# A two-block transformer kernel: the v projection in wide blocks, a later end of the state-space work, and 16 KB more SBUF for expert weights

## Chip, cores, metric

One Trainium2 chip, one core. The metric is the device time of one execution in microseconds (us), the median of three runs. A profile is taken of one further execution of the same program.

## What is computed

256 tokens of width 1024 pass through two blocks, all in 32-bit floats. The first block projects the normed tokens by one matrix `w_in` into eight pieces and runs a state-space branch (SSM) and a dilated attention beside each other:

```python
h = rms_norm(x, norm_w[layer])
proj = h @ w_in[layer].astype(f32)
u_s, z_s, q, k, v, z_a, r_s, r_a = jnp.split(proj, offsets, axis=-1)
y_s = s5_branch(u_s, ...)
y_s = (y_s * jax.nn.silu(z_s)) @ w_ssm_out[layer]
...
y_a = dilated_attention(q, k, v)
y_a = (y_a * jax.nn.silu(z_a)) @ w_attn_out[layer]
m = jax.nn.sigmoid(r_s) * y_s + jax.nn.sigmoid(r_a) * y_a
x = x + m @ w_o[layer]
```

q, k and v are 1536 columns wide. The second block has a gated linear recurrence, a differential attention and then a mixture of experts: 32 experts with three 1024 x 512 matrices each, two experts per token.

## The kernel before, in words

**Two regimes.** Up to about 600 us the dense projections run, then the experts. The dense weights are some 84 MB, the expert weights 192 loads of 1 MB (the last 16 of them in half size, 200 loads in the program).

**Dense weights.** All of them go through one queue of chunks (`stream`, `pull_load`, `pull_split`, `next_weights`). A chunk is 128 x 1024 numbers (512 KB). It is loaded by SP into a slot of WR, and `pull_split` then makes two halves of each number: ScalarE copies the chunk to a rounded type (hi, line 272), VectorE subtracts (lo = w - hi, line 253), each into a slot of WR of the rounded type fp32r. TensorE then takes three products (hi x hi, hi x lo, lo x hi) in place of one in full 32 bits. The keys named in `WHOLE` (before: u, k, v) are not split: `dense` multiplies the chunk as it is, one matmul per tile, which the profile shows as two records each, line 453 `d<-WR,WR`. `dense` works on one block of 256 columns. `dense_wide` (line 477), used for the keys in `WIDE`, works on two blocks at once with 512 columns per matmul; its 48 matmuls read four chunks. WR has five slots, one of 1024 columns and four of 2048, so nine places for a chunk; `make` changes a free slot's type. Two of the slots begin as 32-bit, three as fp32r.

**Work beside the projections.** SSM, the preparation of q and k (`head_prep`) and the attention are generators. `side_run` pulls them on between the chunks at the rates in `SIDE`. `side_drain` finishes one of them at the place in `ORDER` that names it: `"ssm"` stands before `"zs"`. SSM goes through four rounds (B = 0 to 3); each has three places where TensorE takes part: transposes (line 764), products with u2 (line 779), and bd and the outputs (lines 819, 833, 836). VectorE does most of the rest with instructions of 504 to 512 columns, among them scans (line 801). The order in which instructions of one engine stand is then fixed by the scheduler of the language.

**Expert weights.** `moe_load` takes the next tile of 1 MB (8 KB of each partition) if a heap has room, else it returns. While the dense projections run, `prefetch` calls it at rates `PFR` until `PF` tiles are held; later it takes all the room there is: the main heap F, a piece of the small heaps, K, four slots R and four of WR. Each group of four experts (`NG`) reads 24 tiles, eight of w1, w3 and w2 each, and gives them back four at a time (line 1867 issues the load into the room that came free).

Of the kernel before, what the change touches and what calls it, by code (L numbers as in the profile page):

```python
# [9 lines left out]
F32 = mybir.dt.float32  # L10
F32R = mybir.dt.float32r
I32 = mybir.dt.int32
AF = mybir.ActivationFunctionType
# [227 lines left out]
class Kernel:  # L241
# [781 lines left out]
    def setup(self):  # L1023
        nc, I = self.nc, self.I
        self.side, self.mid = [], []
        self.mheaps = [self.F]
        self.moe_stream()
        self.depth_load, self.depth_split = 3, 2
        self.pf_due, self.pf_rate, self.pf_limit = 0.0, 0.6, 0
        self.ring = Ring(self.keepp.tile([128, RING_COLS], F32, name="ring"), RING_COLS)  # L1030
        self.cst = self.keepp.tile([128, C_KEEP], F32, name="cst")
        self.prm = self.keepp.tile([128, P_KEEP], F32, name="prm")
        self.cst2, self.prm2 = self.K.alloc(NC_CONST - C_KEEP), self.K.alloc(NC_PAR - P_KEEP)
        self.K.sq = self.K.alloc(128)
        sq = Ring(self.K.sq.ap, 128)
        self.sq = {n: sq.take(w) for n, w in (("q", 48), ("k", 48), ("dq", 16), ("dk", 16))}
        self.epsb = self.keepp.tile([128, 1], F32, name="epsb")
        self.V.memset(self.epsb, EPS)
        self.act(self.small(1), self.epsb, AF.Tanh)
        nc.sync.dma_start(self.prm, I["prm"][:, :P_KEEP])  # L1040
        self.ident = self.con("ident")
        self.u_dram = nc.dram_tensor("u_scratch", [DM, T], F32, kind="Internal").ap()

    def first_block(self):
        nc, I, F, R = self.nc, self.I, self.F, self.R
# [60 lines left out]
        hT = []  # L1106
# [17 lines left out]
        nc.sync.dma_start(self.cst[:, 128:], I["cst"][:, 128:C_KEEP])  # L1124
        self.pull_split(raw(1))
        next(tables)
        one = self.one = self.keepp.tile([128, 1], F32, name="one")
        V.memset(one, 1.0)
        ss = self.psum("o", 2)

# [20 lines left out]
        for c in range(4):  # L1151
            ev = evac_to(uT)(c)
# [23 lines left out]
        ssm = self.ssm(u2, uT)  # L1176
# [27 lines left out]
        def shaped_ps(ps):  # L1204
            return ps.rearrange("p t (h d) -> p t h d", d=64)
# [14 lines left out]
        def last(which, c):  # L1220

            if which == WHOLE[-1] and c == 5:
                hT.extend((R.alloc(8, 256), R.alloc(8, 256)))
                self.mid.extend(halves(i) for i in range(4))

        def operand(which):
            return (hr, None) if which in WHOLE else hT

        att = None
        for which in ORDER[1:ORDER.index("so")]:  # L1230
            if which not in WHOLE:
                ssm_side[1] = SIDE[6]
            if which in ("k", "q"):
                raw = big[which]
                raw.ap = shaped(raw.ap, (12, 2, 128))
                sq = self.sq[which]
                if which in WHOLE:
                    for c in range(6):
                        last(which, c)
                        self.dense(which, *operand(which), heads(c, raw, sq), token_major=True)  # L1240
                else:
                    for c in range(3):
                        self.dense_wide(which, *hT, heads2(c, raw, sq))
                preps[which] = self.head_prep(which, raw.ap, sq)
                self.side_add(preps[which], SIDE[1])
                trans[which] = raw
            elif which == "v":
                v = big["v"]
                v.ap = shaped(v.ap, (2, 24, 64))
                for c in range(6):  # L1250
                    def ev(ps, c=c):
                        self.scaled_tok(v[:, :, c * 4:c * 4 + 4], shaped_ps(ps))
                    last("v", c)
                    self.dense("v", *operand("v"), ev, token_major=True)
            elif which in width:
                g = gate[which] = F.alloc(width[which], 256)
                for c in range(width[which] // 2):
                    self.dense(which, hT[0], hT[1], (silu2 if which[0] == "z" else tanh_half)(g, c))
                if which == LAST_H:
                    for b in (*hT, self.rows):  # L1260
                        b.free()
                    self.rows = None
            elif which == "mask":
                self.amask = F.alloc(1024)
                nc.sync.dma_start(self.amask.ap, I["amask"])
            elif which == "att":
                for n in "qk":
                    self.side_drain(preps[n])
                for n in "qk":
                    self.show(n + "T", trans[n].ap.rearrange("p m t d -> p m (t d)"))  # L1270
                ao = F.alloc(4, 256)
                att = self.attention(trans["q"], trans["k"], v, gate["za"], ao)
                self.side_add(att, SIDE[2])
            elif which == "ssm":
                self.side_drain(ssm)
                for b in self.m3 + self.bbp + [self.bd, self.d0, self.stab] + self.ptab + self.hst + [u2, uT]:
                    b.free()
                self.show("y2", self.g_hi.ap.bitcast(F32))
            elif which == "attend":
                self.side_drain(att)  # L1280
                for b in (trans["q"], trans["k"], v, gate["za"], self.amask):
                    b.free()
                self.show("att", ao.ap)
            elif which == "ao":
                a_hi, a_lo = R.alloc(4, 256), R.alloc(4, 256)
                for hp in range(4):
                    self.split(a_hi[:, hp], a_lo[:, hp], ao[:, hp])
                ao.free()
                ra = gate["ra"]
                for c in range(4):  # L1290
                    def ev(ps, c=c):
                        w = slice(2 * c, 2 * c + 2)
                        self.stt(ra[:, w], ra[:, w], 1.0, ps, ALU.add, ALU.mult)
                    self.dense("ao", a_hi, a_lo, ev, k=4)
                a_hi.free()
                a_lo.free()
            elif which == "glu":
                zs = gate["zs"]
                s_hi, s_lo = R.alloc(8, 256), R.alloc(8, 256)
                for c in range(4):  # L1300
                    def ev(ps, c=c):
                        w = slice(2 * c, 2 * c + 2)
                        t, y = self.E.alloc(2, 256), self.E.alloc(2, 256)
                        self.act(t.ap, ps, AF.Tanh, scale=0.25)
                        self.add(y.ap, self.g_hi[:, w].bitcast(F32), self.g_lo[:, w].bitcast(F32))
                        self.stt(t.ap, t.ap, 1.0, y.ap, ALU.add, ALU.mult)
                        self.mul(t.ap, t.ap, zs[:, w])
                        self.split(s_hi[:, w], s_lo[:, w], t.ap)
                        t.free()
                        y.free()  # L1310
                    self.dense("glu", self.g_hi, self.g_lo, ev)
                self.g_hi.free()
                self.g_lo.free()
                zs.free()
        xn = F.alloc(2, DM, low=True)
        nc.sync.dma_start(xn.ap, I["x"].rearrange("(b p) d -> p b d", p=128))
        rs = gate["rs"]
# [290 lines left out]
    def second_block(self):  # L1608
        nc, I, F, R = self.nc, self.I, self.F, self.R
# [9 lines left out]
            self.sub(e[:, i], lb[:, i], mx)  # L1619
        e2 = self.small(8, name="lbe2")  # L1620
        self.exp_small(e2, e.rearrange("p a b -> p (a b)"))
        half = self.keepp.tile([128, 4], F32, name="half")
        nhalf = self.keepp.tile([128, 4], F32, name="nhalf")
        self.add(half, e2[:, 0:4], e2[:, 4:8])
        V.reciprocal(half, half)
        self.mul(half, half, e2[:, 0:4])
# [3 lines left out]
        hT = self.hT2  # L1630
# [58 lines left out]
        dv = F.alloc(2, 512)  # L1689
# [107 lines left out]
        for tb in range(2):  # L1797
            ps = self.psum("d", 2, 256)[:, 0]
            one = slice(tb, tb + 1)
# [416 lines left out]


START = 2
WHOLE = ("u", "k", "v")
WARM = (2, 7)  # L2220
SIDE = (5.2, 1.2, 2.5, 2.7, 2.4, 3.4, 3.2)
PAIRED = ("hf",)
WIDE = ("q", "hi", "dq", "dk", "dv", "wo2")
ORDER = ("u", "k", "v", "q", "mask", "za", "ra", "att", "ssm", "zs", "rs", "glu", "attend", "ao", "so", "wo")
LAST_H = "rs"
PF = (5, 6, 9, 20)
PFR = (0.4, 0.5, 0.6, 1.0)
HEAPS = (("F", 108), ("E", 6), ("FS", 12), ("K", 8))
RING_COLS = 432


def lay(inputs):
# [19 lines left out]
    for name, key in (("w_in", "w_in"), ("w_glu", "w_glu"), ("w_ao", "w_attn_out"), ("w_so", "w_ssm_out"), ("w_wo", "w_o"),  # L2252
                      ("w_in_2", "w_in_2"), ("w_bh", "w_branch_hg_2"), ("w_bd", "w_branch_da_2"), ("w_wo2", "w_out_2")):
        A[name] = chunks(f[key][0])
    for name, blocks in (("w_in", (8, 10, 12)), ("w_wo", (0, 2)), ("w_in_2", (4, 8, 10, 12)), ("w_wo2", (0,))):
        for c in blocks:
            two = A[name][c:c + 2]
            A[name][c:c + 2] = two.transpose(1, 2, 0, 3).reshape(two.shape)
    for name, key in (("w1", "w1_2"), ("w3", "w3_2"), ("w2", "w2_2")):
        w = f[key][0]  # L2260
        e, k, n = w.shape
# [56 lines left out]
```

## Time and profile before

| | us |
|---|---|
| median of three runs (1053.07 to 1053.28) | 1053.15 |
| the profiled execution, its own time | 1052.02 |
| span of the profiled execution, first to last instruction | 1050.2 |
| TensorE busy | 943.1 |
| VectorE busy | 511.4 |
| ScalarE busy | 338.8 |

Of the span, TensorE (PE) is busy 90%, VectorE (DVE) 49%, ScalarE (ACT) 32%. The page cuts the span into 40 slices of 26.25 us and gives for each the busy tenths of every engine, TensorE's granted clock (PEclk) and what the 16 DMA engines moved. HBM was read for 290.98 MB. The section with the rows below says for each group which view it is.

### The profile page before, as it was taken

How to read it: one execution, taken by the hardware profiler on the slowest of the kernel's cores; microseconds unless marked ns; L12 is line 12 of the kernel's file. 1: busy time of each engine (PE TensorE's matmuls, PEld its weight loads, DVE VectorE, ACT ScalarE, POOL GpSimd, SP SyncE). 2: the span in 40 equal slices, each digit the busy share in tenths (PEclk: the TensorE clock that was granted, in tenths of full speed). 3: DMA queues.
4: the chain of work that ended last, by engine and by line, in shares of the span. 5: the costliest groups of instructions: out<-in, count | busy, mean ns of one | idle time of the engine just before them, and what ended most of it. 6: DMA issues, size and time to landing. Idle time of an engine off the chain costs nothing.

```text
span 1050.2 us, 16534 instructions
## 1 busy us (share of the span) xinstructions
PE 943.1 (90%) x6771; PEld 653.7 (62%) x6771; DVE 511.4 (49%) x1154; ACT 338.8 (32%) x580; POOL 11.7 (1%) x39
## 2 busy tenths in 40 slices
PE   8999999999999999999999999877869687787875
PEld 6888887999999989988899844231313122131212
DVE  8977885978767778695768521010101001010102
ACT  3343557456554456454644411000010000000000
POOL 2000000000000000000000010000000000000000
PEclk9999999999999999998999999998999899998978
DMA  7854354554437664653559999999999999999996
GB/s 255 200 182 124 119 186 137 181 181 127 136 106 230 215 231 154 193 175 110 173 168 322 357 395 422 420 421 420 422 421 422 421 422 420 421 422 422 422 416 238
DMA packets 61459, 294.24 MB, mean 280 GB/s; under 512 B 10944, under 2 KB 13376, under 8 KB 37824
## 3 DMA queue, kind: packets, MB, share of 16 engines
q1 hardware_dynamic: 61376, 293.11, 74.3%
q8 instruction: 55, 0.90, 0.4%
q14 instruction: 28, 0.23, 0.1%
HBM read 290.98 MB, written 2.10 MB: 279 GB/s over the span
## 4 chain that ended last, share of the span: by engine, by line
PE 52%; DMA 40%; DVE 4%; ACT 2%; issue 1%; SPq 0%; POOL 0%; DVEq 0%; ACTq 0%
DMA heap<-in_w_dram 32%; PE d L453 31%; PE d L477 9%; DMA R<-in_w_dram 4%; DMA heap<-in_w_last_dram 2%; DMA WR<-in_w_dram 2%; DVE WR L253 1%; DVE heap L253 1%; PE d L502 1%; PE s L925 1%; PE h L1981 1%; ACT heap L272 1%; PE s L944 1%; PE o L959 1%; PE s L836 1%
## 5 line engine op out<-in xcount | busy, mean ns | idle before, releaser
L453 PE MATMUL d<-R,WR 128*128 128x256 f32 x1920 | 241.4, 285 | 3.1 <-DVE WR L253 2.3
L453 PEld LDWEIGHTS d<-R,WR 128*128 128x128 f32 x1920 | 232.9, 191 | 8.9 <-DVE WR L253 3.7
L1981 PE MATMUL h<-heap 128*32 128x512 f32 x736 | 161.6, 665 | 43.3 <-DMA heap<-in_w_dram 42.6
L253 DVE TENSOR_TENSOR WR<-WR,WR 128x1024 fp32r<-128x1024 f32 x128 | 156.5, 1223 | 61.1 <-ACT WR L272 55.8
L272 ACT ACTIVATE WR<-WR 128x1024 fp32r<-128x1024 f32 x128 | 135.3, 1057 | 137.5 <-PE d L453 65.7
L1981 PEld LDWEIGHTS h<-heap 128*32 128x32 f32 x736 | 35.3, 119 | 139.7 <-DMA heap<-in_w_dram 77.5
L477 PE MATMUL d<-WR,R 128*128 128x512 f32 x480 | 115.9, 397 | 0.2 <-DVE heap L269 0.2
L453 PE MATMUL d<-WR,WR 128*128 128x256 f32 x512 | 113.6, 381 | 2.4 <-DMA WR<-in_w_in_dram 2.3
L253 DVE TENSOR_TENSOR heap<-heap 128x512 f32<-128x512 f32 (+7 forms) x250 | 108.4, 481 | 3.1 <-ACT heap L272 1.6
L453 PEld LDWEIGHTS d<-WR,WR 128*128 128x128 f32 x512 | 96.2, 190 | 17.6 <-ACT heap L272 2.8
L477 PEld LDWEIGHTS d<-WR,R 128*128 128x128 f32 x480 | 89.3, 190 | 20.3 <-ACT heap L272 0.8
L2013 PE MATMUL r<-heap 128*32 128x512 f32 (+1 forms) x328 | 87.4, 546 | 15.1 <-DMA heap<-in_w_dram 14.4
L1981 PE MATMUL h<-R,heap 128*32 128x512 f32 x240 | 89.4, 710 | 11.9 <-DMA R<-in_w_dram 11.6
L272 ACT ACTIVATE heap<-heap 128x512 f32<-128x512 f32 (+4 forms) x133 | 68.9, 529 | 70.4 <-DVE heap L253 19.7
L269 DVE SCALAR_TENSOR_TENSOR WR<-r,ring,WR 128x512 fp32r<-128x512 f32 (+1 forms) x18 | 12.4, 692 | 136.4 <-ACT WR L272 136.4
L2013 PEld LDWEIGHTS r<-heap 128*32 128x32 f32 x328 | 20.5, 109 | 70.4 <-DMA heap<-in_w_dram 37.6
L253 DVE TENSOR_TENSOR heap<-heap,h 128x512 f32<-128x512 f32 x8 | 5.5, 688 | 119.2 <-PE h L1981 119.1
L2013 PE MATMUL r<-WR,heap 128*32 128x512 f32 (+1 forms) x232 | 58.3, 555 | 5.4 <-ACT heap L272 4.8
L272 ACT ACTIVATE WR<-r,ring 128x512 fp32r<-128x512 f32 (+1 forms) x18 | 11.5, 640 | 124.8 <-PE r L2013 113.4
L269 DVE SCALAR_TENSOR_TENSOR heap<-heap,h 128x512 f32<-128x512 f32 x8 | 5.5, 688 | 94.8 <-ACT heap L272 94.8
L272 ACT ACTIVATE heap<-h,ring 128x512 f32<-128x512 f32 x8 | 5.5, 688 | 142.7 <-PE h L1981 131.2
L1981 PEld LDWEIGHTS h<-R,heap 128*32 128x32 f32 x240 | 18.4, 126 | 34.8 <-DMA R<-in_w_dram 25.1
(218 smaller groups left out, 854.5 us busy)
## 6 DMA issues: line engine op xcount, KB each, us to landing
heap<-in_w_dram SPq DMA_DIRECT2D x123, 1024.0 KB, 19.8
WR<-in_w_in_dram SPq DMA_DIRECT2D x114, 512.0 KB, 3.8
R<-in_w_dram SPq DMA_DIRECT2D x32, 1024.0 KB, 19.8
WR<-in_w_dram SPq DMA_DIRECT2D x29, 1024.0 KB, 19.9
WR<-in_w_wo_dram SPq DMA_DIRECT2D x16, 512.0 KB, 4.9
heap<-in_w_last_dram SPq DMA_DIRECT2D x10, 512.0 KB, 10.2
WR<-in_w_glu_dram SPq DMA_DIRECT2D x8, 512.0 KB, 3.6
WR<-in_w_so_dram SPq DMA_DIRECT2D x8, 512.0 KB, 4.7
```

The source lines that it names most:

```text
L253: (eng or self.V).tensor_tensor(out=out, in0=a, in1=b, op=op)
L269: self.V.scalar_tensor_tensor(out=out, in0=a, scalar=s, in1=b, op0=op0, op1=op1)
L272: self.A.activation(out, a, func, **kw)
L453: self.PE.matmul(ps[:, j], lhsT, rhs, start=h == 0 and i == 0 and n == 0, stop=h == k - 4 and kk == 3 and n == len(terms) - 1, skip_group_ ...
L477: self.PE.matmul(ps[tb], x[:, h + kk, sl], w[:, kk], start=h == 0 and kk == 0 and n == 0, stop=h == 6 and kk == 1 and n == 2)
L502: self.PE.matmul(ps[c][:, j], lhsT, rhs, start=h == 0 and i == 0 and n == 0, stop=h == 4 and kk == 3 and n == 2, skip_group_check=True)
L836: PE.matmul(py[:, d * 64:], self.bd[:, bl, d], uT[:, blk, :256 - 64 * d], start=False, stop=d == 3, skip_group_check=True)
L925: PE.matmul(ps[hh][:, cols], qT[r, q, qs], kT[r, q, k], start=True, stop=True)
L944: PE.transpose(pt[:, kb], s[:, kb * 128:(kb + 1) * 128], self.ident)
L959: PE.matmul(po[hp][r, qb], v[:, tb, g * 8 + hp * 2 + hh], ts_[hh][:, kb], start=kb == 0, stop=kb == 3)
L1981: PE.matmul(ph[sl[g]], xg[:, kk, sl[g]], w(name, kk // 4, g)[:, kk % 4], start=kk == 0, stop=kk == 7)
L2013: PE.matmul(pys[c][sl[g]], hT[:, kk, sl[g]], rhs, start=kk == 0, stop=kk == 3)
```

## The change

Four things, in one diff:

1. `"v"` leaves `WHOLE` and joins `WIDE`: its weights are laid out in pairs of blocks, split into hi and lo, and multiplied by `dense_wide` in three wide blocks in place of six blocks of 256 columns. The halves hT of the tokens are made at the end of k rather than of v.
2. `"ssm"` stands after `"zs"` in `ORDER`, and SSM's rate is 6.6 (from 5.2) while the `WHOLE` keys run and 2.5 (from 3.2) after them.
3. `dynamic_dma_scratch_size=64` frees 16 KB of each partition, and heap F grows from 108 to 124 units of 1 KB. Small tiles are merged to make it fit.
4. `PF` and `PFR` allow more expert tiles earlier.

```diff
@@ -1247,11 +1248,11 @@
             elif which == "v":
                 v = big["v"]
                 v.ap = shaped(v.ap, (2, 24, 64))
-                for c in range(6):
-                    def ev(ps, c=c):
-                        self.scaled_tok(v[:, :, c * 4:c * 4 + 4], shaped_ps(ps))
-                    last("v", c)
-                    self.dense("v", *operand("v"), ev, token_major=True)
+                for c in range(3):
+                    def ev(ps, tb, c=c):
+                        self.act(v[:, tb, c * 8:c * 8 + 8], ps.rearrange("p (h d) -> p h d", d=64), AF.Copy,
+                                 scale=self.rstd[:, tb:tb + 1])
+                    self.dense_wide("v", *hT, ev)
...
-WHOLE = ("u", "k", "v")
+WHOLE = ("u", "k")
 WARM = (2, 7)
-SIDE = (5.2, 1.2, 2.5, 2.7, 2.4, 3.4, 3.2)
+SIDE = (6.6, 1.2, 2.5, 2.7, 2.4, 3.4, 2.5)
 PAIRED = ("hf",)
-WIDE = ("q", "hi", "dq", "dk", "dv", "wo2")
-ORDER = ("u", "k", "v", "q", "mask", "za", "ra", "att", "ssm", "zs", "rs", "glu", "attend", "ao", "so", "wo")
+WIDE = ("v", "q", "hi", "dq", "dk", "dv", "wo2")
+ORDER = ("u", "k", "v", "q", "mask", "za", "ra", "att", "zs", "ssm", "rs", "glu", "attend", "ao", "so", "wo")
 LAST_H = "rs"
-PF = (5, 6, 9, 20)
-PFR = (0.4, 0.5, 0.6, 1.0)
-HEAPS = (("F", 108), ("E", 6), ("FS", 12), ("K", 8))
+PF = (7, 8, 12, 22)
+PFR = (0.5, 0.6, 0.8, 1.0)
+HEAPS = (("F", 124), ("E", 6), ("FS", 12), ("K", 8))
...
-    nc = bacc.Bacc("TRN2", target_bir_lowering=False, num_devices=1)
+    nc = bacc.Bacc("TRN2", target_bir_lowering=False, num_devices=1, dynamic_dma_scratch_size=64)
```

What it moves is told by the built program. On VectorE, before, the first splits are those of q's chunks (names: `WR_67<-WR_111,WR_67` is lo out of the loaded chunk in WR_111; `s_1151` is the PSUM tile of line 779), between operations of SSM's third round:

```order
L253 TENSOR_TENSOR WR_67<-WR_97,WR_67 128x1024
L253 TENSOR_TENSOR heap<-heap 128x512 x5
L253 TENSOR_TENSOR heap<-s_1151,heap 128x2x4x64 x2
L253 TENSOR_TENSOR heap<-heap 128x512
L253 TENSOR_TENSOR heap<-s_1151,heap 128x2x4x64 x2
L801 SCALAR_TENSOR_TENSOR heap<-heap 128x512
L253 TENSOR_TENSOR heap<-heap 128x512
L253 TENSOR_TENSOR WR_1211<-WR_111,WR_1211 128x1024
L801 SCALAR_TENSOR_TENSOR heap<-heap 128x512
L253 TENSOR_TENSOR heap<-heap 128x8x63 x3
L253 TENSOR_TENSOR WR_67<-WR_111,WR_67 128x1024
```

With the change, the same engine at the second to fourth chunk of v, where SSM's second round and the first steps of k's preparation (128x48) stand between the splits:

```order
L253 TENSOR_TENSOR heap<-s_800,heap 128x2x4x64 x2
L801 SCALAR_TENSOR_TENSOR heap<-heap 128x512
L253 TENSOR_TENSOR heap<-heap 128x512
L253 TENSOR_TENSOR WR_852<-WR_97,WR_851 128x1024
L801 SCALAR_TENSOR_TENSOR heap<-heap 128x512
L1189 TENSOR_REDUCE heap<-heap 128x8
L253 TENSOR_TENSOR WR_67<-WR_97,WR_852 128x1024
L253 TENSOR_TENSOR heap<-heap 128x8x63 x2
L266 TENSOR_SCALAR ring<-heap 128x48
L253 TENSOR_TENSOR WR_851<-WR_111,WR_67 128x1024
```

Twelve splits are new, and the splits begin one stage and one SSM round earlier. They also use other slots: before, fp32r tiles are two slots (four places), and the loads have five; now fp32r has three slots (67, 851, 852: five places) and the loads four (97, 111).

On SP, near the load of the router's matrix (`in_router`), which is where the second block's gates end, before:

```order
L1867 DMA heap_58<-in_w3_dram 128x2048
L382 DMA WR1_64<-in_w_in_2_dram 128x1024
L382 DMA WR3_111<-in_w_in_2_dram 128x1024 x2
L382 DMA WR0_63<-in_w_in_2_dram 128x1024
L382 DMA WR1_64<-in_w_in_2_dram 128x1024 x2
L382 DMA WR3_111<-in_w_in_2_dram 128x1024
L1740 DMA heap_58<-in_router_dram 128x288
L382 DMA WR3_111<-in_w_bh_dram 128x1024
```

and with the change:

```order
L1868 DMA heap_58<-in_w3_dram 128x2048
L382 DMA WR2_97<-in_w_bh_dram 128x1024 x2
L382 DMA WR3_111<-in_w_bh_dram 128x1024
L382 DMA WR3_111<-in_w_bd_dram 128x1024
L382 DMA WR2_97<-in_w_bd_dram 128x1024
L1868 DMA heap_58<-in_w3_dram 128x2048
L382 DMA WR2_97<-in_w_bd_dram 128x1024
L1741 DMA heap_58<-in_router_dram 128x288
L1868 DMA heap_58<-in_w3_dram 128x2048
```

Seven expert tiles stand ahead of the router's load before, eleven now. Ahead of the first load that needs room given back by an expert group, 22 tiles stand before and 24 now.

## Rows read from the trace of the kernel before

**Rows 1.** The page: span; TensorE's busy tenths and DMA's rate in 40 slices.

```profile
span 1050.2 us, 16534 instructions
...
PE   8999999999999999999999999877869687787875
...
GB/s 255 200 182 124 119 186 137 181 181 127 136 106 230 215 231 154 193 175 110 173 168 322 357 395 422 420 421 420 422 421 422 421 422 420 421 422 422 422 416 238
```

**Rows 2.** The chain that ended last, in order of time: start, us, what.

```profile
614.85 7.07 PE h L1981 x64
622.32 16.52 DMA heap<-in_w_dram
...
1038.83 1.93 PE r L2013 x26
```

**Rows 3.** Busy time by window: from:to us, then PE, PEld, DVE, ACT, POOL; PEclk, DMA share, GB/s.

```profile
88.00:139.00 51.00, 51.00 (x510) 44.24 (x509) 43.64 (x86) 17.35 (x41) 0.00 (x0) 1.00 0.42 134
139.00:185.00 46.00, 45.05 (x419) 36.20 (x417) 31.92 (x42) 33.57 (x57) 0.00 (x0) 1.00 0.50 158
```

**Rows 4.** The same view, at the hand-over to the experts and within them.

```profile
590.00:595.00 5.00, 5.00 (x46) 5.00 (x45) 2.51 (x6) 2.70 (x7) 0.00 (x0) 1.00 0.55 185
...
610.00:615.00 5.00, 5.00 (x48) 2.67 (x44) 0.11 (x1) 0.63 (x2) 0.00 (x0) 1.00 0.73 270
660.00:1030.00 370.00, 285.61 (x1488) 90.63 (x1484) 33.32 (x95) 24.38 (x46) 0.00 (x0) 0.94 1.01 421
```

**Rows 5.** TensorE in order of time: start, us, line, out<-in, count of records.

```profile
107.09 1.12 PE L819 MATMUL s<-heap 128*32 128x128 f32 x32
...
111.79 1.10 PE L833 MATMUL s<-heap 128*32 128x64 f32 x64
112.82 1.42 PE L836 MATMUL s<-heap 128*128 128x256 f32 x8
...
116.45 14.03 PE L453 MATMUL d<-WR,WR 128*128 128x256 f32 x64
130.31 1.04 PE L764 MATMUL s<-cst,heap 128*128 128x128 f32 x8
...
134.74 1.16 PE L779 MATMUL s<-heap 64*64 64x64 f32 x64
...
365.20 11.10 PE L477 MATMUL d<-WR,R 128*128 128x512 f32 x48
```

**Rows 6.** Groups of instructions by line and form: busy, mean ns | idle before, releaser.

```profile
L253 DVE TENSOR_TENSOR WR<-WR,WR 128x1024 fp32r<-128x1024 f32 x128 | 156.5, 1223 | 61.1 <-ACT WR L272 55.8 <-PE o L959 3.3 <-PE s L764 1.5
L272 ACT ACTIVATE WR<-WR 128x1024 fp32r<-128x1024 f32 x128 | 135.3, 1057 | 137.5 <-PE d L453 65.7 <-PE d L477 32.9 <-issue 22.4
L253 DVE TENSOR_TENSOR heap<-heap 128x512 f32<-128x512 f32 x97 | 64.5, 684 | 2.9 <-ACT heap L272 1.6 <-PE s L764 0.8
L269 DVE SCALAR_TENSOR_TENSOR heap<-heap 128x256 f32<-128x256 f32 x24 | 11.8, 490 | 7.1 <-ACT heap L272 6.9
L801 DVE TENSOR_TENSOR_SCAN heap<-heap 128x512 f32<-128x512 f32 x8 | 9.7, 1217 | 0.0
L253 DVE TENSOR_TENSOR heap<-heap,ring 128x1536 f32<-128x1536 f32 x4 | 7.0, 1749 | 0.0
L253 DVE TENSOR_TENSOR heap<-heap,rc 128x192 f32<-128x192 f32 x8 | 2.8, 352 | 0.1
L253 DVE TENSOR_TENSOR ring<-ring 128x48 f32<-128x48 f32 x6 | 1.2, 203 | 0.1
L453 PEld LDWEIGHTS d<-R,WR 128*128 128x128 f32 x1920 | 232.9, 191 | 8.9 <-DVE WR L253 3.7 <-issue 2.4 <-DVE R L253 0.8
```

**Rows 7.** VectorE in order of time, with idle time before and its releaser in brackets.

```profile
41.37 6.10 DVE L253 TENSOR_TENSOR heap<-heap 128x512 f32<-128x512 f32 x10
...
60.48 0.69 DVE L1188 TENSOR_REDUCE heap<-heap 128x8 f32<-128x512 f32 x1 [5.05 <-ACT heap L272]
...
89.30 0.69 DVE L1188 TENSOR_REDUCE heap<-heap 128x8 f32<-128x512 f32 x1 [3.79 <-ACT heap L272]
```

**Rows 8.** SP's DMA queue in order of time, late in the experts.

```profile
953.79 17.72 SPq L1867 DMA_DIRECT2D heap<-in_w_dram x8
```

More of the change, by code (lines that the diff above doesn't have):

```diff
@@ L1036, in setup @@
         self.sq = {n: sq.take(w) for n, w in (("q", 48), ("k", 48), ("dq", 16), ("dk", 16))}
-        self.epsb = self.keepp.tile([128, 1], F32, name="epsb")
+        ones = self.keepp.tile([128, 2], F32, name="ones")
+        self.epsb, self.one = ones[:, 0:1], ones[:, 1:2]
         self.V.memset(self.epsb, EPS)
@@ L1126, in first_block @@
         next(tables)
-        one = self.one = self.keepp.tile([128, 1], F32, name="one")
+        one = self.one
         V.memset(one, 1.0)
@@ L1621, in second_block @@
         self.exp_small(e2, e.rearrange("p a b -> p (a b)"))
-        half = self.keepp.tile([128, 4], F32, name="half")
-        nhalf = self.keepp.tile([128, 4], F32, name="nhalf")
+        both = self.keepp.tile([128, 8], F32, name="half")
+        half, nhalf = both[:, 0:4], both[:, 4:8]
         self.add(half, e2[:, 0:4], e2[:, 4:8])
@@ L2254, in lay @@
         A[name] = chunks(f[key][0])
-    for name, blocks in (("w_in", (8, 10, 12)), ("w_wo", (0, 2)), ("w_in_2", (4, 8, 10, 12)), ("w_wo2", (0,))):
+    for name, blocks in (("w_in", (8, 10, 12, 20, 22, 24)), ("w_wo", (0, 2)), ("w_in_2", (4, 8, 10, 12)), ("w_wo2", (0,))):
         for c in blocks:
```

## Prediction

> **What bounds the kernel now.** I read the page's slices first. TensorE fills every slice up to about 600 us, while DMA moves between 106 and 255 GB/s there; from the 25th slice on DMA moves 416 to 422 GB/s (but for the last) and TensorE has gaps [rows 1]. So there are two regimes, and the chain in order of time shows the seam: the last long TensorE piece is the experts' first matmuls (7.07 us at 614.85), and from 622.32 on the chain is expert loads one behind another, up to the matmuls of 1.93 us at 1038.83 [rows 2]. In the experts TensorE is busy 285.61 of 370 us and DMA moves 421 GB/s in all of them [rows 4].
>
> The end is therefore: the moment at which the experts begin to give room back, plus the bytes that are not yet in SBUF at that moment, at 421 GB/s. A us saved on TensorE before the seam is a us saved at the end, and so is each expert tile that is in SBUF earlier. One tile costs 2.48 us: eight loads stand in 17.72 us on SP's queue, of which the last issue takes 0.33, so seven steps in 17.39 [rows 8]; 1.0486 MB at 421 GB/s gives 2.49.
>
> Whether memory or DMA limited the tiles held at the seam is told by the gaps: DMA share 0.55 in 590 to 595 and 0.73 in 610 to 615, then none [rows 4]. In the second gap SP had nothing with a place to go: 22 tiles were held and the first four were still in use. More room is worth something there.
>
> In the stage of v TensorE was busy 51.00 of 51.00 us, VectorE 43.64, ScalarE 17.35 [rows 3]. So v is paid in TensorE time, and VectorE has 7.4 us to spare, no more.
>
> **1. v's matmuls.** Removed: six blocks of 16 matmuls, two records each, 192 records. 64 records take 14.03 us [rows 5], so 42.1 us. Added: three wide blocks of 48 matmuls with 512 columns; 48 of them take 11.10 us [rows 5], so 33.3 us. Gain 8.8 us on TensorE, all of it on the path.
>
> **2. The splits of v.** Twelve chunks more are split: 12 x 1.057 = 12.7 us of ScalarE and 12 x 1.223 = 14.7 us of VectorE [rows 6]. ScalarE has the room (17.35 of 51) and also has what it had for v's results, so I take 0 for it; its cover is the same 33.3 us of matmuls. VectorE is close. From the first split of v to the last, the changed order has 87 VectorE instructions: the 12 splits (14.7 us), 30 of 504 or 512 columns at 0.684 (20.5), 2 scans at 1.217 (2.4), 2 of 1536 at 1.749 (3.5), 16 of 256 at up to 0.490 (7.8), 14 of 128 or 192 at up to 0.352 (4.9) and 11 of 48 at 0.203 (2.2) [rows 6]: 56.0 us. These means overlap: ten of 512 columns in a row took 6.10 us [rows 7], 0.61 each and 0.074 less than the mean, so with nothing between them the 87 take 49.6 us.
>
> TensorE in that time: v's 33.3 us, and between them in its order one set of line 819 (1.12), two of lines 833 and 836 (2 x 2.52) and eight transposes (1.04) [rows 5], 40.5 us. VectorE also has a lead: its first split of v stands right behind the results for which the first line-833 matmul waits, and between that matmul and v's first one stand 54 records of k (11.8 us), the rest of lines 833 and 836 (5.0), the transposes (1.04) and line 779 (1.16) [rows 5], 19.0 us. In k VectorE waited for ScalarE, 5.05 and 3.79 us [rows 7]; I take such 8.8 us off the lead. So 50.7 us are there for 49.6 to 56.0, and TensorE stalls by 0 to 5.3 us. I take 2.0, nearer to the low end since in v few VectorE rows wait for a result of ScalarE's. The far bound, with no lead, is 56.0 - 40.5 = 15.5.
>
> **3. SSM drawn out, slots changed.** SSM's work is the same in number, only later: its fourth round now stands in zs. The rows of TensorE in it (1.04 + 1.16 + 1.12 + 5.04 = 8.4 us a round) are paid wherever they stand: 0. The hi and lo tiles have five places in place of four, so that ScalarE can make the next hi while TensorE still reads both older pairs; the loads have four in place of five, three of which are filled ahead. TensorE's weight loads waited 3.7 us for VectorE's splits over the whole dense part [rows 6]: at best these 3.7 us come back, at worst as much again is lost by loads that find their place later. I take 0.
>
> **4. 16 KB more.** That is two tiles (24 in place of 22 held before the first release). They replace 2 x 2.48 = 5.0 us at the end. To be in time they must be loaded before the seam; the idle of the two gaps alone is 0.45 x 5 + 0.27 x 5 = 3.6 us, which bounds the gain from below if they are loaded only then. But eleven tiles in place of seven are ahead of the router's load in SP's order, in a part in which DMA moved 110 to 193 GB/s [rows 1]; so I take 5.0. The expert loads that are moved ahead stand before dense loads on SP's queue, at most one or two together, each 2.48 us; the dense chunks are issued three ahead, some 8 us of matmuls (11.10 us for four chunks [rows 5]), so I cost that at nothing. If this cover is gone, a dense chunk is late and TensorE waits for a load.
>
> **Sum.** -8.8 + 2.0 + 0 - 5.0 = -11.8 us. The profiled execution took 1052.02 us (span 1050.2 and 1.8 around it), 1.1 below the median of 1053.15. It would become 1040.2, the median 1041.4.
>
> **A rule against it.** In v VectorE was busy 43.64 of 51 us and TensorE's weight loads 44.24 [rows 3]. The Trainium skill, Trace Analysis, "Identifying the Most-Contended Engine", takes busy share as a fair measure for VectorE, tells to judge TensorE by its weight loads, and names the engine with the highest share as the one to relieve; by that, v is already nearly VectorE's, and the change loads VectorE by 14.7 us more. That is the first rival. I hold against it that TensorE had no idle in the window and VectorE had, and that the lead is worth 10 us.
>
> **Rivals.**
> *VectorE sets v.* The lead is worth nothing and the stall is the far bound, 15.5 us: the seam moves by -8.8 + 15.5 = +6.7, two tiles give 5.0 back, 1054.9. For it: the sum of 56.0 us of VectorE work in 40.5 of TensorE's. Against: the 19.0 us of lead. It decides when most of the lead is gone.
> *Slower.* VectorE's queue is in order and a split in it waits for ScalarE's hi, which waits for TensorE to leave the slot: VectorE idled 55.8 us before splits in that way, ScalarE 65.7 [rows 6]. If that idle is kept whole in the stretch from k to zs, added VectorE work lengthens it in full: the seam moves by +14.7 and not by -8.8, and 5.0 come back: 1062.9. SSM's matmuls, which stand in TensorE's queue ahead of projections, would be where TensorE waits. It makes the kernel slower from a stall of 13.8 us on. Against: VectorE's idle in v was not at splits at all, and the fifth place takes ScalarE's copy out of the wait.
> *The stall eats the gain.* A stall of 8.8 us: the seam stays, two tiles count, 1048.1. For it: the same sums, half the lead.
> *Memory does nothing.* The tiles come late or a release, not room, sets the start: -8.8 + 2.0 alone, 1046.4. Against: the gap at 610 to 615.
> *More than the sum.* No stall in v and the 3.7 us of split waits come back: -8.8 - 3.7 - 5.0 = -17.5, 1035.7. For it: the fifth place.
>
> **Chances.** My forecast (a stall in v up to 5 us, tiles worth 3.6 to 5.0; 1039 to 1046): 0.63. More than the sum: 0.10. Memory does nothing: 0.08. The stall eats the gain: 0.09. VectorE sets v: 0.04. Slower: 0.06. A measurement of this kernel tells 0.2%, 2.1 us, from no change, so 1051.0 to 1055.3 is "same": faster 0.90 (the first four), same 0.04, slower 0.06. The range of 8 in 10 runs from 1037.5 to 1048.5: the forecast with the bounds of the stall and the tiles, the case without memory, the stall that eats the gain, and the near half of the better case.
>
> **What would show it.** v's stage: 144 records of line 477 more, in some 40.5 us plus the stall, with TensorE's idle there released by VectorE at splits; over 5 us of it means the lead was over-counted. The last dense matmul some 6.8 us earlier than before. A wider DMA gap right before the experts' first release, then 421 GB/s without a gap and with the same length for 24 tiles. If the experts' first matmuls come 6.8 us earlier and the end does too, with no more, the memory was worth nothing. Wrong altogether: TensorE waiting in za to zs for SSM's results, or for dense loads behind expert tiles.

## The result, and the profile after

| | before | after |
|---|---|---|
| median (us) | 1053.22 (1053.07 to 1053.39, 4 runs) | 1038.71 (1038.15 to 1038.78, 4 runs) |
| the profiled execution, its own time | 1052.02 | 1038.15 |
| span | 1050.2 | 1036.4 |

The ratio is 0.9863 (95% interval 0.985 to 0.9876), so 14.4 us less; 11.8 were forecast. Where they came from is read in the same order as before.

The page after: the span, TensorE's busy tenths and DMA's rate in 40 slices (now 25.9 us each), to be held against [rows 1].

```profile
span 1036.4 us, 16567 instructions
...
PE   9999999999999999999999999877868787776875
...
GB/s 253 221 171 140 145 163 144 169 180 177 149 129 239 229 216 164 197 181 89 184 197 333 328 391 421 421 421 421 421 421 421 421 421 421 421 420 421 421 417 255
```

The two regimes are as they were. The chain in order of time (start, us, what) gives the seam:

```profile
606.62 10.44 PE h L1982 x96
...
645.71 20.95 DMA WR<-in_w_dram
...
1026.64 1.93 PE r L2014 x26
```

The experts' first long matmuls start at 606.62 and not at 614.85 [rows 2]: 8.2 us of the gain lie before the seam (6.8 were forecast). From there to the end of the span it is 429.8 us, where it was 435.3: 5.6 us come from the experts (5.0 were forecast). This is one profile: a second one of the same program, from the run that repeats the change, has the experts' first long matmuls at 603.79 and a span of 1032.6, so 11.1 and 6.5 us. The chain hangs on loads only from 645.71 on, before from 622.32.

Busy time by window (columns as in [rows 3]), within the experts:

```profile
660.00:1020.00 360.00, 276.30 (x1466) 89.38 (x1465) 32.84 (x93) 24.25 (x46) 0.00 (x0) 0.94 1.01 420
```

The experts run at the same rate as before. For DMA's gaps at the hand-over the windows have to lie alike to the experts' first long matmuls, which now come 8.2 us earlier: from 30 us before them to 10 behind, and the 8 us around them, in the kernel before and then with the change:

```profile
584.85:624.85 40.00, 39.27 (x312) 26.40 (x310) 15.04 (x66) 8.36 (x22) 3.38 (x15) 1.00 0.91 366
610.85:618.85 8.00, 8.00 (x76) 3.58 (x72) 1.39 (x6) 0.63 (x2) 0.00 (x0) 1.00 0.83 327
```

```profile
576.62:616.62 40.00, 39.26 (x309) 26.18 (x307) 15.05 (x66) 7.92 (x24) 3.38 (x15) 1.00 0.92 358
602.62:610.62 8.00, 8.00 (x76) 3.58 (x72) 1.39 (x6) 0.62 (x2) 0.00 (x0) 1.00 0.86 325
```

DMA's gaps are as they were: a share of 0.91 and 0.92 in the 40 us, of 0.83 and 0.86 in the 8.

TensorE in order of time, from k into v (idle before, and its releaser, in brackets):

```profile
72.45 0.43 PE L833 MATMUL s<-heap 128*32 128x64 f32 x16 [1.79 <-DVE heap L253]
...
87.37 0.34 PE L779 MATMUL s<-heap 64*64 64x64 f32 x8 [0.64 <-ACT heap L272]
88.16 1.04 PE L779 MATMUL s<-heap 64*64 64x64 f32 x56 [0.45 <-ACT heap L272]
...
92.51 5.83 PE L477 MATMUL d<-WR,R 128*128 128x512 f32 x24
...
112.62 8.46 PE L477 MATMUL d<-WR,R 128*128 128x512 f32 x36
...
122.12 8.24 PE L477 MATMUL d<-WR,R 128*128 128x512 f32 x35 [0.93 <-ACT heap L272]
```

v's wide matmuls take 33.8 to 35 us (144 at 8.46 for 36 or 5.83 for 24). The 144 records stand from 92.51 to some 133.1, 40.6 us with the matmuls of SSM between them; 40.5 plus the stall were forecast. No wait of TensorE in v is for a split. The waits over 0.4 us in k and v are 1.79, 0.64, 0.45 and 0.93, 3.8 us. The first three stand in k and are for SSM's results. The fourth stands ahead of v's third wide block. The two PSUM tiles (where matmuls leave their results) that `dense_wide` takes are the only two named `d`, and ScalarE comes to the second block's result only then (ScalarE in order of time):

```profile
121.39 1.25 ACT L272 ACTIVATE heap<-d,rstd 128x512 f32<-128x512 f32 x2
```

So 2.9 us are waits for SSM, and 0.93 is a wait for v's own result to be taken away.

The last groups that matter, by line and form (columns as in [rows 6]):

```profile
L453 PEld LDWEIGHTS d<-R,WR 128*128 128x128 f32 x1920 | 232.8, 192 | 5.2 <-issue 2.6 <-DVE WR L253 0.5 <-ACT R L272 0.3
L477 PEld LDWEIGHTS d<-WR,R 128*128 128x128 f32 x624 | 116.1, 189 | 27.7 <-ACT heap L272 1.7 <-DVE WR L253 1.4 <-DVE heap L269 0.4
L253 DVE TENSOR_TENSOR WR<-WR,WR 128x1024 fp32r<-128x1024 f32 x140 | 171.1, 1223 | 72.4 <-PE d L453 20.7 <-issue 20.5 <-PE d L477 19.7
```

Here stands what I had set to 0. The weight loads of line 453 waited 3.7 us for splits [rows 6], now 0.5; with the 1.4 of line 477, which had none, 1.9 are left. And VectorE before its splits no longer waits for ScalarE's hi (55.8 us before), but for TensorE to leave a place.

So the open questions were: is v's gain held down by VectorE or by anything else; is it the fifth place that took the split waits away; does drawing SSM out cost the waits in k and v; and is the memory worth its two tiles?

### The profile page after: what moved, and what is told of

The parts are those of the page before. It is cut to its first block, busy times and chain, and to the rows that moved or that the text cites. A ratio compares the mean times of both kernels' runs of the same rounds, so it can differ in the third digit from the quotient of the medians.

```text
span 1036.4 us, 16567 instructions
## 1 busy us (share of the span) xinstructions
PE 932.3 (90%) x6723; PEld 644.8 (62%) x6723; DVE 521.0 (50%) x1166; ACT 352.1 (34%) x586; POOL 11.6 (1%) x39
## 4 chain that ended last, share of the span: by engine, by line
PE 54%; DMA 37%; DVE 6%; ACT 2%; issue 1%; POOL 0%; SPq 0%; DVEq 0%; ACTq 0%
PE d L453 27%; DMA heap<-in_w_dram 23%; PE d L477 12%; DMA WR<-in_w_dram 12%; DVE heap L253 3%; PE h L1982 2%; DMA WR<-in_w_last_dram 2%; DVE WR L253 1%; ACT heap L272 1%; PE d L502 1%; PE s L925 1%; PE r L2014 1%; PE o L959 1%; PE s L944 1%; PE d L1804 1%
## 5 line engine op out<-in xcount | busy, mean ns | idle before, releaser
L1982 PE MATMUL h<-heap 128*32 128x512 f32 x1024 | 179.3, 675 | 61.0 <-DMA heap<-in_w_dram 60.1
L477 PE MATMUL d<-WR,R 128*128 128x512 f32 x624 | 149.5, 396 | 1.9 <-DVE WR L253 1.0
L477 PEld LDWEIGHTS d<-WR,R 128*128 128x128 f32 x624 | 116.1, 189 | 27.7 <-ACT heap L272 1.7
L272 ACT ACTIVATE heap<-heap 128x512 f32<-128x512 f32 (+5 forms) x133 | 68.8, 531 | 60.6 <-DVE heap L253 28.5
L2014 PE MATMUL r<-WR,heap 128*32 128x512 f32 (+1 forms) x288 | 79.3, 550 | 10.8 <-DMA WR<-in_w_dram 9.9
L2014 PE MATMUL r<-R,heap 128*32 128x512 f32 (+1 forms) x288 | 69.8, 551 | 9.0 <-ACT heap L272 4.8
L453 PE MATMUL d<-WR,WR 128*128 128x256 f32 x320 | 73.1, 388 | 1.1 <-ACT heap L272 1.1
L453 PEld LDWEIGHTS d<-WR,WR 128*128 128x128 f32 x320 | 61.5, 194 | 11.5 <-ACT heap L272 2.6
L2014 PEld LDWEIGHTS r<-WR,heap 128*32 128x32 f32 x288 | 19.0, 109 | 56.5 <-DMA WR<-in_w_dram 27.0
L2014 PEld LDWEIGHTS r<-R,heap 128*32 128x32 f32 x288 | 14.6, 109 | 36.0 <-issue 15.5
```

What stands on the lines that cost most here:

```text
L272: self.A.activation(out, a, func, **kw)
L453: self.PE.matmul(ps[:, j], lhsT, rhs, start=h == 0 and i == 0 and n == 0, stop=h == k - 4 and kk == 3 and n == len(terms) - 1, skip_group_ ...
L477: self.PE.matmul(ps[tb], x[:, h + kk, sl], w[:, kk], start=h == 0 and kk == 0 and n == 0, stop=h == 6 and kk == 1 and n == 2)
L1982: PE.matmul(ph[sl[g]], xg[:, kk, sl[g]], w(name, kk // 4, g)[:, kk % 4], start=kk == 0, stop=kk == 7)
L2014: PE.matmul(pys[c][sl[g]], hT[:, kk, sl[g]], rhs, start=kk == 0, stop=kk == 3)
```

## Experiments

Twelve runs, compared by their ratios to runs of the kernel before on the same chip (their median 1052.48, 1052.54 and 1051.56 us in the three sets of four).

| run | median, us | ratio (95%) | us less |
|---|---|---|---|
| change again | 1038.70 | 0.9869 (0.9853 to 0.9886) | 13.8 |
| memory alone | 1047.08 | 0.9947 (0.9934 to 0.9961) | 5.6 |
| change, 16 KB withheld | 1045.02 | 0.9923 (0.9909 to 0.9936) | 8.1 |
| change, 8 KB withheld | 1041.25 | 0.9905 (0.989 to 0.992) | 10.0 |
| change, old prefetch limits | 1038.29 | 0.9879 (0.9864 to 0.9894) | 12.7 |
| change, v without lo | 1039.21 | 0.9873 (0.9858 to 0.9888) | 13.4 |
| change, four places for hi and lo | 1042.68 | 0.9909 (0.9892 to 0.9926) | 9.6 |
| change, six places | 1044.53 | 0.9937 (0.9923 to 0.995) | 6.6 |
| change, SSM as before | 1036.56 | 0.9847 (0.9834 to 0.9861) | 16.1 |
| the same again | 1037.36 | 0.9855 (0.9838 to 0.9871) | 15.3 |
| change, old rates, late drain | 1036.44 | 0.9858 (0.9843 to 0.9873) | 15.0 |
| change, new rates, old drain | 1039.43 | 0.9859 (0.9836 to 0.9883) | 14.8 |

"Us less" is one minus the ratio, times 1053.2. The change itself, by its two measurements (14.4 and 13.8), stands at 14.1.

**Memory.** The kernel before with the 16 KB, the merged tiles and the new limits:

```diff
-HEAPS = (("F", 108), ("E", 6), ("FS", 12), ("K", 8))
+HEAPS = (("F", 124), ("E", 6), ("FS", 12), ("K", 8))
...
-PF = (5, 6, 9, 20)
+PF = (7, 8, 12, 22)
...
-    nc = bacc.Bacc("TRN2", target_bir_lowering=False, num_devices=1)
+    nc = bacc.Bacc("TRN2", target_bir_lowering=False, num_devices=1, dynamic_dma_scratch_size=64)
```

> The kernel before with nothing but the 16 KB for heap F (merged small tiles, small descriptor scratch) and the new prefetch limits; v, SSM and the order as before. Theory: two tiles of 2.48 us, 1053.2 - 5.0 to 5.6 = 1047.6 to 1048.2, with the seam where it was. Rival (the room pays only when the seam moves, or the tiles are late): 1051 to 1053.

The change with 16 KB taken out of heap F again, from the second block on (`self.withheld = F.alloc(4096, top=True)`, old `PF` and `PFR`):

> The changed kernel, but at the start of the second block a tile of 16 KB per partition is taken from heap F and never given back, and the old prefetch limits stand: v in wide blocks and the late SSM alone, 22 expert tiles held. Theory (end = seam + bytes not yet held): the seam stays where the change put it, 8.2 us earlier than before, and the two tiles are lost: 1038.7 + 5.0 to 5.6 = 1043.7 to 1044.3. Rival (the seam's gain needs the room too, since fewer loads crowd the dense chunks, or the room is worth more than its bytes): over 1045.5, or under 1042.

And with half of it taken out (`F.alloc(2048, top=True)`, `PF = (6, 7, 11, 21)`):

> The changed kernel with 8 KB of heap F withheld from the second block on, so that 23 expert tiles are held at the seam in place of 24 (with 16 KB withheld it took 6.3 us more). Theory A (each tile is its own bytes at the end, 2.48 us, and a little of gaps): 2.5 to 3.5 us slower than the changed kernel, 1041.2 to 1042.2. Rival B (24 is a whole group of four experts, and the gain comes with the last of them): most of the 6.3 us is lost already with one, over 4.5 us. Rival C (the first tile is worth little, the second much): under 1.5 us.

Alone the memory gives 5.6 us; taken out of the change it costs 6.0. The traces part it more finely, since the seam stays put in three of them. Span, and the first matmul of the experts' routing on TensorE, in the kernel after, then with 8 KB and with 16 KB withheld:

```profile
span 1036.4 us, 16567 instructions
597.73 0.25 PE L1928 MATMUL h<-WR,O 128*128 128x32 f32 x1
```

```profile
span 1038.7 us, 16501 instructions
597.53 0.25 PE L1929 MATMUL h<-WR,O 128*128 128x32 f32 x1
```

```profile
span 1043.0 us, 16511 instructions
597.63 0.25 PE L1929 MATMUL h<-WR,O 128*128 128x32 f32 x1
```

From there to the end 438.7, 441.2 and 445.4 us: the first tile withheld costs 2.5, the second 4.2. The eleven profiles of kernels with 24 tiles lie between 437.7 and 438.9 there, so the 2.5 stands for 2.3 to 3.5. Against the sum's 2.48 each the pair is worth 1.7 more; in the device times the first costs 4.1 with an interval of about 1.8 to either side. That it is the tiles' own bytes (theory A) and not the completeness of the first group (rival B) rests on the trace's 2.5. The same stretch is 444.2 us in the kernel before and 437.7 with memory alone, 6.5 less; that run's routing starts 1.6 us later than before, so that the two spans differ by 4.9 only. Why two tiles are worth 6.5 to 6.7 and not 5.0 is not shown.

The limits alone (heap F kept at 124, `PF` and `PFR` as before, six tiles ahead of the router's load in place of eleven):

> The changed kernel with the prefetch limits and rates of before, so that 24 tiles still have room but fewer (6 in place of 11) stand ahead of the router's load. Theory A (all 24 are in SBUF by the first release anyway, since DMA has gaps before the seam): within 1 us of the changed kernel. Rival B (the tiles that are asked for late come late): 1.4 to 2.5 us slower, with a DMA share nearer to 1 in the last 15 us before the seam. Rival C (the earlier tiles delayed dense chunks): 0.5 to 1.5 us faster before the seam.

1.4 us more than the change by the ratio, with an interval that takes in 0; its phase from the routing on is 438.3 us, no longer than the change's. So the order of the early tiles is worth nothing that shows: it is room that counts.

**VectorE in v.** VectorE's lo for v left out; ScalarE copies eight columns in its place, and the third product takes hi:

```diff
+            if key == "v":
+                self.act(lo[:, 0, :8], w[:, 0, :8], AF.Copy)
+            else:
+                self.sub(lo.ap, w.ap, hi.ap.bitcast(F32))
-                    for n, (w, x) in enumerate(((hi, x_hi), (hi, x_lo), (lo, x_hi))):
+                    for n, (w, x) in enumerate(((hi, x_hi), (hi, x_lo), (hi if key == "v" else lo, x_hi))):
```

> The changed kernel without VectorE's subtraction for v's twelve chunks: lo is not computed (the third product takes hi again, same matmuls; ScalarE touches eight columns of lo). It leaves out the low part of v's weights. VectorE is relieved of 14.7 us in v. Theory (TensorE stalls by 1 to 2.5 us in v): 1036.2 to 1037.7. Rival (VectorE sets the pace of v): 5 us or more come back, under 1033.7. Rival (no stall is VectorE's): 1038.7.

v's stage and the first 8 us of q by window, in the change and then without VectorE's lo:

```profile
92.00:141.00 49.00, 48.07 (x364) 39.13 (x364) 47.79 (x84) 30.48 (x49) 0.00 (x0) 1.00 0.53 162
```

```profile
93.00:141.00 48.00, 47.73 (x362) 38.84 (x361) 35.93 (x72) 31.17 (x59) 0.00 (x0) 1.00 0.49 165
```

VectorE falls from 47.79 busy us of 49 to 35.93 of 48, and the time gains nothing. By TensorE's order of time v and q take 83.6 us there and 84.3 in the change. VectorE was full, but it did not set the pace.

**The places.** The hi and lo tiles kept out of slot 0 of WR, so that they have four places and the loads five:

```diff
+            if self.name == "WR" and i == 0 and dt == F32R and not low:
+                continue
```

> The changed kernel with the hi and lo tiles kept out of one slot, so that they have four places and the loads five, as before the change. Theory A: the fifth place is what brought back the waits of TensorE's weight loads for splits (3.1 us of idle for them in the page before, 0.4 in the page after): 1.5 to 3 us slower than the changed kernel. Rival B: those waits went because the splits moved to other neighbours on VectorE: within 0.7 us. Rival C: five places for loads are worth more than five for the halves: up to 2 us faster.

4.5 us of the change's 14.1 are gone. Groups by line and form (the edit moves line numbers by two):

```profile
L455 PEld LDWEIGHTS d<-R,WR 128*128 128x128 f32 x1920 | 232.9, 191 | 7.7 <-DVE WR L255 2.5 <-issue 2.4 <-DVE R L255 0.8
L479 PEld LDWEIGHTS d<-WR,R 128*128 128x128 f32 x624 | 116.2, 191 | 28.8 <-DVE WR L255 2.5 <-issue 1.1 <-ACT heap L274 0.9
L255 DVE TENSOR_TENSOR WR<-WR,WR 128x1024 fp32r<-128x1024 f32 x140 | 171.0, 1221 | 56.6 <-ACT WR L274 53.1 <-PE o L961 3.3
```

The split waits are back (2.5 and 2.5 us for 0.5 and 1.4), and VectorE follows ScalarE again (53.1 us). By TensorE's order of time v and q take 86.7 us in place of 84.3, and za to the first matmul of `wo` 182.2 in place of 180.3. v's own 144 records take 40.9 us there, with 1.0 us of weight loads waiting for splits, and 40.6 in the change, with the 0.93 for ScalarE; so nearly all of the loss comes behind v. So the change of the slots is worth some 4 us, spread over the dense part.

Then one place more, and one less for the loads (slots 1, 2 and 4 for hi and lo, 0 and 3 for loads, once the first chunk is split):

```diff
+            if self.name == "WR" and i in (0, 3) and dt == F32R and not low:
+                continue
+            if self.name == "WR" and dt == F32 and size == 1024 and not low and (i == 2 or i in (1, 4) and self.split):
+                continue
...
```

> The changed kernel with six places for the hi and lo tiles and three for the loads (as the change has it: five and four). With four and five it had become 4.0 us slower. Theory A (the number of places for the halves is what TensorE waits for): a sixth place brings a little more, but little is left to bring back, since weight loads wait 0.4 us for splits in the page of the changed kernel: 0 to 1 us faster, 1037.7 to 1038.7. Rival B (three places for loads make chunks late): TensorE waits for DMA in the dense part, 1 to 5 us slower. Rival C (the four-place run was slow for its five load places and not for its four places of halves): then three load places are faster still, by over 1.5 us.

7.5 us slower than the change, more than any theory had. ScalarE in order of time, in v and q, then TensorE, SP's DMA queue, and VectorE's splits as a group:

```profile
100.47 1.06 ACT L276 ACTIVATE WR<-WR 128x1024 fp32r<-128x1024 f32 x1 [1.17 <-DMA WR<-in_w_in_dram]
...
135.96 1.06 ACT L276 ACTIVATE WR<-WR 128x1024 fp32r<-128x1024 f32 x1 [1.70 <-DMA WR<-in_w_in_dram]
136.92 0.67 ACT L276 ACTIVATE heap<-d,rstd 128x512 f32<-128x512 f32 x1
```

```profile
137.65 1.64 PE L486 MATMUL d<-WR,R 128*128 128x512 f32 x6 [1.17 <-ACT heap L276]
```

```profile
85.01 0.33 SPq L1275 DMA_DIRECT2D heap<-in_amask_dram  x1
96.58 32.89 SPq L386 DMA_DIRECT2D WR<-in_w_in_dram  x11
```

```profile
L257 DVE TENSOR_TENSOR WR<-WR,WR 128x1024 fp32r<-128x1024 f32 x140 | 171.2, 1223 | 58.6 <-ACT WR L276 52.9 <-PE o L968 5.0 <-ACT heap L276 0.3
```

SP issues no load for 11 us, and two splits wait for their chunks; in the change no split waits for one between 84 and 180 us. Behind the second of them ScalarE is late with a result of v, and TensorE waits 1.17 us for it. This speaks for rival B, whose price (1 to 5 us) was put too low. VectorE waits 52.9 us for ScalarE before its splits here too, as with four. That hi and lo of a chunk lie in one slot with four places is not the reason: with six they share one in 47 of 140 chunks, with five in 56, by the built programs. No run parted the three load places from the six others, so B is likely and not shown. Shown is that theory A, more places for the halves the better, is false, and that five and four is the best of the three ways tried to part the nine.

**SSM drawn out.** The change with `SIDE` and `ORDER` as before:

```diff
-SIDE = (6.6, 1.2, 2.5, 2.7, 2.4, 3.4, 2.5)
+SIDE = (5.2, 1.2, 2.5, 2.7, 2.4, 3.4, 3.2)
-ORDER = ("u", "k", "v", "q", "mask", "za", "ra", "att", "zs", "ssm", ...)
+ORDER = ("u", "k", "v", "q", "mask", "za", "ra", "att", "ssm", "zs", ...)
```

> The changed kernel with SSM as before (drained before zs, rates 5.2 and 3.2): v in wide blocks, the room, no drawing out. Theory: where SSM's work stands costs nothing while VectorE has time to spare, so 1038.7 within 1.0. Rival (VectorE is so close in v and q that SSM had to be drawn out): with a rate of 3.2 in v TensorE waits for splits 4 to 8 us more, 1042.5 to 1046.5.

It came out a little lower than expected, and a second set with the change beside it was to tell whether that holds, and which of the two lines it is:

> The changed kernel unaltered, as the pair of the three runs beside it. Expected 1038.2 us (1037.5 to 1039), if this chip gives the kernel before some 1052.5 to 1053 again; the sum over the earlier runs gives nothing else. If it comes out below 1037.5, the differences of the earlier runs (1036.56 for SSM as before) were partly the chip's.

> The changed kernel with SSM's place and rates as they were before the change (ssm ahead of zs, 5.2 and 3.2). Theory A: the higher rate in k makes TensorE wait there for results of VectorE and ScalarE (1.79 + 0.64 + 0.45 + 0.93 us in the changed kernel's trace against 0.49, 1.05 and 0.20 without), so drawing SSM out costs some 2 us: 1036.0 to 1037.0, 1.5 to 2 below the changed kernel on the same chip. Rival B: the first run of this kernel was 2 us low by accident of the clock in the recurrence: equal to the changed kernel within 0.7 us.

> The changed kernel with SSM drained ahead of zs as before, but with the new rates 6.6 and 2.5. It parts the rate from the place. Theory A (the rate in k costs): the waits in k stay, within 0.7 us of the changed kernel. Rival B (the late place costs, since SSM's results then come when zs wants them): 1.5 to 2 us below it, as with both parts undone. Rival C (neither costs): all three equal.

> The changed kernel with the rates of SSM as before (5.2 and 3.2) but its drain behind zs, the fourth corner beside the changed kernel (both new), both old, and new rates with the old drain. Theory A (the rate in k costs some 1.5 us, the place nothing): equal to both old, 1036.5 to 1037.5. Rival B (the late place costs): equal to the changed kernel, 1038.2 to 1039. The scatter of single runs (about 2 us) is as large as the difference, so only all four corners together can tell, two against two.

In both sets the kernel with SSM as before is the faster, by 1.7 and 1.5 us; the mean of the two differences, 1.6, has an interval of about 1.7. TensorE in order of time in that kernel (its first profile) shows shorter waits in k:

```profile
71.28 0.43 PE L833 MATMUL s<-heap 128*32 128x64 f32 x16 [0.49 <-DVE heap L253]
...
74.25 0.99 PE L833 MATMUL s<-heap 128*32 128x64 f32 x56 [1.05 <-DVE heap L253]
```

The waits of 0.2 us and more in k and v sum to 3.8 and 4.0 us in the two profiles of the change and 3.4 with the new rates alone, but to 1.5 to 1.7 in the three profiles with the old rates. So the rate of 6.6 makes TensorE wait some 2 us more, 1.3 in k for SSM and 0.9 in v for ScalarE to take v's result away; that is shown by six profiles of four kernels. The times don't part the two lines: the three measurements at the new rates average 0.9864 and the three at the old ones 0.9853, the three with the late drain 0.9863 and the three with the early one 0.9854, some 1 us each, and a single one of them has an interval of 0.0014 to 0.0024 to either side. The traces speak for the rate: the first matmul of `wo` comes at 356.0, 357.1 and 358.5 us with the new rates, the last of them with the early drain, and at 354.4, 355.0 and 355.9 with the old ones, the middle one with the late drain. The means are 357.2 and 355.1, and the late place shows no cost.

## Why the prediction was right, step by step

The time lay 2.7 us below the forecast, within the range of 8 in 10 and just under the forecast's own 1039 to 1046. The sum held because its two large terms did; the terms for the waits did not hold as put, and that they missed in both directions is luck.

- *v's matmuls, -8.8.* Right. 33.8 to 35 us stand in place of 42.1 (33.3 forecast). Of the 40.6 us of v's stage some 6.4 are SSM's matmuls and 0.93 is the wait, which leaves 33.3. With SSM as before, the first matmul of za comes at 174.9 and 176.3 us in two profiles, before at 185.1: 8.8 to 10.2 us, the fifth place included, so what v gains arrives.
- *The stall from the splits, +2.0.* Mis-sized. "v's stage ... with TensorE's idle there released by VectorE at splits" is wrong: v has one idle of 0.93 us, released by ScalarE, which is late with v's own result, and the other 2.9 us stand in k, in front of SSM's matmuls. That they sum to something near 2.0 is chance. VectorE's load was well summed: 49.6 to 56.0 us were forecast from the first split of v to the last, and it is busy 48.76 there, in 53.32 us, so the lead covered it:

```profile
75.80:129.12 53.32, 51.31 (x546) 42.42 (x536) 48.76 (x89) 33.12 (x58) 0.00 (x0) 1.00 0.47 147
```

- *SSM drawn out, slots changed, 0.* Here the sum was mis-sized. Behind "I take 0" two effects were hidden: the parting of the places gives some 4 us (four places cost 4.5), and the drawn-out SSM takes about 1.6. That "at best these 3.7 us come back" named the right mechanism, though by the rows about half of them did (1.9 us of split waits are left, 5.0 with four places); I set it to 0 without a row that spoke for 0. The rival "more than the sum" was half right for that reason.
- *16 KB, -5.0.* Nearly right: 5.6 alone, 6.0 within the change, and 6.5 and 6.7 by the stretch from the routing on.
- *The gap before the first release.* "A wider DMA gap" did not come; laid at the seam, it is as it was (0.83 and 0.86). So the room is worth its bytes and more, but the gap that was read as the sign for it did not move; where the two loads found their time is not parted.

From runs: memory -5.6, places -4.5, SSM +1.6; what is left of -14.1 for v with four places is -5.6, 3 less than its 8.8. That remainder was not run by itself and carries the intervals of all the others. The trace of the run with four places does not put it into v, which takes 40.9 us there: the loss lies in q and from za to `wo`, and the fifth place takes it away. That it is v's splits that crowd those behind them is likely and not shown.

The rule against the change was told ahead: the Trainium skill, Trace Analysis, "Identifying the Most-Contended Engine", takes the engine with the highest busy share as the one to relieve. The runs go against it here: in v and the start of q VectorE stood at 47.79 of 49 us, and relieving it of 12 us moved the time by nothing that shows. The same page's "Optimization Strategy" says that bubbles which repeat can mean too few buffers for the next tile; the four-place run agrees with that (5.0 us of split waits for 1.9), the six-place run shows that more is not by itself better.

The rivals in which VectorE sets v, the stall eats the gain, or the memory does nothing are excluded by the runs without lo and with memory alone. The slower one, in-order queues kept waiting by splits, lives on only in the places: VectorE's 53 us of waiting for ScalarE stand there with four and with six. TensorE waiting in za to zs, the sign of being wrong altogether, did not come: from za to 260 us its longest wait is 0.33.

No run is faster than the change by a margin that the intervals clear; SSM as before is the likeliest to be (15.3 and 16.1 us less than before, against 13.8 and 14.4).

## What to carry to other kernels

An engine that is full for a stage does not set its pace while it has a lead over the one that waits for it; sum the work up to the point where it is due, and then take the waits by their releaser, not by the busy share. Where one pool of slots serves both loads and converted tiles, how it is parted can be worth half as much as a stage's arithmetic (4 us here against 8.8), and here the best of three ways lay between the other two: try one place to either side. When a kernel ends in a phase bound by memory, count the tiles held when it starts: each was worth at least its bytes at the full rate here, however early it was loaded.

## What had not been expected of the hardware

The same program varied more than thought: the change again ran from 1034.34 to 1039.65 us. Two of its profiles differ by 3.8 us, and one place is plain. In the recurrence of the second block TensorE's granted clock falls while TensorE is busy without a gap, in a run of small matmuls. Windows of the change's two profiles (columns as in [rows 3]; first the one shown above):

```profile
465.00:470.00 5.00, 5.00 (x35) 4.17 (x35) 3.70 (x6) 0.00 (x0) 0.00 (x0) 0.77 0.56 185
470.00:475.00 5.00, 5.00 (x19) 4.28 (x20) 0.00 (x0) 2.23 (x4) 0.00 (x0) 0.55 0.01 5
```

```profile
465.00:470.00 5.00, 5.00 (x39) 4.36 (x38) 2.62 (x5) 0.00 (x0) 0.00 (x0) 0.87 0.38 120
470.00:475.00 5.00, 5.00 (x25) 4.20 (x24) 1.23 (x1) 4.06 (x7) 0.00 (x0) 0.79 0.00 0
```

A share of 0.55 means nearly all of the stretch at the lower level (1.2 of 2.4 GHz). TensorE in order of time in the first of the two, before and in the fall:

```profile
466.63 0.44 PE L1438 MATMUL s<-heap 64*128 64x64 f32 x4
467.00 0.66 PE L1442 MATMUL s<-heap 128*128 128x64 f32 x4
...
469.18 0.69 PE L1438 MATMUL s<-heap 64*128 64x64 f32 x4
469.81 1.11 PE L1442 MATMUL s<-heap 128*128 128x64 f32 x4
...
472.34 4.02 PE L477 MATMUL d<-WR,R 128*128 128x512 f32 x12
```

Four matmuls of line 1442 take 0.66 us and then 1.11, and twelve wide ones 4.02 where 3.01 to 3.02 is usual in q. In the second profile the fall comes later, and from the first matmul of `hi` to line 1464 behind this run it is 1.5 us shorter (70.1 for 71.6). From the first matmul of `wo` to that of the routing, where most of them run the same code, the profiles of the two kernels and the twelve runs take 238.9 to 242.3 us; the longest, with new rates and the old drain, has a granted clock of 0.50 and 0.59 in the two windows from 470 to 480. So a few us of scatter are made there, whatever is changed elsewhere, and differences of 1 to 2 us between two single runs say nothing here.
